# A two-layer encoder's first feed-forward matrices: one weight sum of each seven-product tile made by an adding DMA, and a fourth such tile in the second call of every group

## The chip, the core and the metric

The kernel runs on one core of a Trainium2 chip. The metric is the device time of one launch in microseconds. PE is TensorE (matmuls; PEld is its weight load), DVE is VectorE, ACT is ScalarE, POOL is GpSimd and SP is SyncE, whose queue issues the loads. A DMA issued from SP's or ACT's queue is generated in hardware, one from POOL's queue in software; the profile lists the latter as queue q0.

## The reference, cut to what matters

```python
for i in range(2):                                   # x: 256 tokens x 2048, float32
    x = x + attention_i(rms_norm(x, mixer_norm_i))   # neighbourhood, then dilated
    g, w1, w2 = ffns[i]                              # w1: 2048 x 8192, w2: 8192 x 2048
    x = x + square(relu(rms_norm(x, g) @ w1)) @ w2
return rms_norm(x, final_norm)
```

The two feed-forward layers (w1 and w2 of each) are most of the work, and the change lies in the product with w1.

## The kernel before

**Arithmetic.** Every float32 factor is split in two parts, hi and lo, both in a rounded 32-bit type: hi is ACT's cast, lo is DVE's difference of the value and hi. A product is three matmuls (`three`, L194 to L196): hi x hi, hi x lo, lo x hi, each 128x128 against 128x512.

**Calls, steps and tiles.** `gemm_pair` multiplies the 256 tokens by 1024 columns of a weight matrix in eight steps, one for each 256 rows of the weights. The step's weights lie in a tile `w` of 128 x 4 x 512: `w[:, 2:4]` are two 128-row blocks of the first 512 columns, `w[:, 0:2]` the same of the second 512. A step is of one of two kinds:
- an s step does eight block products, 24 matmuls;
- an x step treats the 2 x 2 blocks in the manner of Strassen and Winograd with seven products, 21 matmuls. It needs three sums of weight blocks more than the sum that takes a block's place, and sums of the token factor, called S1 to S4.

A feed-forward layer has four groups `g`. Each has two calls on w1 (`cp` 0 and 1, the first and the second) and two on w2. Which steps are x is written out by `ff_order`: a w1 call has x at pairs 2, 4 and 6; the first call of groups 1 to 3 (`more`) also at pair 5, in the order 0, 1, 2, 5, 3, 4, 6, 7. Calls on w2 have two to four x steps.

**Queues and their order.** The program is one long loop over the steps, in an order written out by hand; each engine runs its instructions in that order. In step i PE works through four quarters; behind quarter n the loop issues, for step i + 2, `prep(i + 2, n)`; at the end of the step SP gets the load of step i + 5, which has to wait until the tile of step i + 2, in the same buffer, has been read. There are three `w` buffers. The parts `wh` and `wl` (hi and lo) have four buffers each, two of them for a step, so that the split of step i + 2 writes where PE reads in step i.

For an s step, `prep` splits `w[:, 2:4]` at n = 1 and `w[:, 0:2]` at n = 3. For an x step `prep_x` does, in this order:
- n = 0, DVE: `sums[0:2]` from `w[1:3]` and `w[0]`, then `sums[2]`, then the sum of all four, written over `w[0]` (L166 to L168, by `add` at L137);
- n = 1: the split of `w[:, 2:4]` (ACT L189, DVE L190), whatever stands in `ahead`, and ACT's cast `hs` of all three sums (L175);
- n = 2, DVE: `ls`, the three sums less `hs` (L178, by `subtract` at L134);
- n = 3: the split of `w[:, 0:2]`.

PE's order in an x step is the list `X`: quarter 0 uses operands 2 and 3 of `s.hi` and `s.lo`, quarter 1 operands 6 and 4, quarter 2 operands 0 and 1, quarter 3 operand 5. Operands 4, 5 and 6 are `hs` and `ls`.

**What else runs beside the steps.** At the end of a call, DVE puts the seven products' sums together (`begin`, `last_sum`). After a w1 call ACT takes the squared ReLU (L790, L791), PE transposes the result in step 1 of the next call (L808), and DVE and ACT split it (`hT`) or make the sums of the token factor from it (`sums_and_parts`). After a w2 call of groups 0 to 2 a DMA from POOL's queue (`bring`, L864) adds C, 1 MB, to x in SBUF.

The adds, the split and the cast of an x step in the code before:

```python
if n == 0:
    add(nc.vector, t[:, 0:2, :], w[:, 1:3, :], w[:, 0, :] ...)
    add(nc.vector, t[:, 2, :], t[:, 1, :], w[:, 1, :])
    add(nc.vector, w[:, 0, :], t[:, 2, :], w[:, 3, :])
elif n == 1:
    split(hi, lo, w[:, 2:4, :])
    ...
    nc.scalar.copy(s.hs, s.sums)
elif n == 2:
    subtract(nc.vector, ls, s.sums, s.hs.bitcast(F32))
```

Of the kernel before, what the change touches and what calls it, by code (L numbers as in the profile page):

```python
# [8 lines left out]
F32 = mybir.dt.float32  # L9
F32R = mybir.dt.float32r  # L10
AF = mybir.ActivationFunctionType
ALU = mybir.AluOpType
AX = mybir.AxisListType

P = 128
# [13 lines left out]
class Step:  # L29
# [6 lines left out]
    def __init__(self, kind, loads, quarters):  # L36
        self.kind = kind
        self.loads = loads
        self.quarters = quarters
        self.evac = []  # L40
        self.after = [[] for _ in range(4)]
        self.tasks = [[] for _ in range(4)]
        self.post = []
        self.ahead = []
        self.hi, self.lo = [None] * 7, [None] * 7


@with_exitstack
def tile_encoder(ctx: ExitStack, tc: tile.TileContext, ins, out):
    nc = tc.nc  # L50
# [12 lines left out]
    x = const.tile([P, 2, D], F32, name="x")  # L63
# [60 lines left out]
    def load(i):  # L124
        if i >= len(steps):
            return
        s = steps[i]
        s.w = wpool.tile([P, 4, 512], F32, name="w", tag="w")
        if i:
            for src, lo, hi in s.loads:  # L130
                nc.sync.dma_start(s.w[:, lo:hi, :], src)

    def subtract(engine, out, a, b):
        engine.tensor_tensor(out=out, in0=a, in1=b, op=ALU.subtract)  # L134

    def add(engine, out, a, b):
        engine.tensor_tensor(out=out, in0=a, in1=b, op=ALU.add)  # L137

    def two_parts(s, u):
        hi = hlpool.tile([P, 2, 512], F32R, name="wh", tag="wh")  # L140
        lo = hlpool.tile([P, 2, 512], F32R, name="wl", tag="wl")
        for a in range(2):
            s.hi[2 * u + a], s.lo[2 * u + a] = hi[:, a, :], lo[:, a, :]
        return hi, lo
# [16 lines left out]
    def prep_x(s, n):  # L161

        w = s.w
        if n == 0:
            t = s.sums = part.pool.tile([P, 3, 512], F32, name="sums", tag="sums", bufs=1)
            add(nc.vector, t[:, 0:2, :], w[:, 1:3, :], w[:, 0, :].unsqueeze(1).to_broadcast([P, 2, 512]))  # L166
            add(nc.vector, t[:, 2, :], t[:, 1, :], w[:, 1, :])
            add(nc.vector, w[:, 0, :], t[:, 2, :], w[:, 3, :])  # L168
        elif n == 1:
            hi, lo = two_parts(s, 1)  # L170
            split(hi, lo, w[:, 2:4, :])
            for f in s.ahead:
                f()
            s.hs = part.pool.tile([P, 3, 512], F32R, name="hs", tag="hs", bufs=2)
            nc.scalar.copy(s.hs, s.sums)  # L175
        elif n == 2:
            ls = part.pool.tile([P, 3, 512], F32R, name="ls", tag="ls", bufs=2)
            subtract(nc.vector, ls, s.sums, s.hs.bitcast(F32))  # L178
            for a in range(3):
                s.hi[4 + a], s.lo[4 + a] = s.hs[:, a, :], ls[:, a, :]  # L180
        else:
            hi, lo = two_parts(s, 0)
            split(hi, lo, w[:, 0:2, :])
# [4 lines left out]
    def split(dst_hi, dst_lo, src):  # L188
        nc.scalar.copy(dst_hi, src)  # L189
        nc.vector.tensor_tensor(out=dst_lo, in0=src, in1=dst_hi.bitcast(F32), op=ALU.subtract)  # L190
# [88 lines left out]
    QUARTERS = (0, 0), (1, 0), (1, 1), (0, 1)  # L279
    STD = {(0, 0): "2", (0, 1): "3", (1, 0): "4", (1, 1): "S"}  # L280

    def gemm_pair(w, cols, A, sums_of, order, finish, split_end=False, soon=False, negated=False):
        made, q = [], {}
        first_x = [n for n, o in enumerate(order) if o[0] == "x"]
        touched = set()

        def left(pair, which):

            t, u = A[pair // 2], 2 * (pair % 2)
            if pair in sums_of and which in sums_of[pair]:  # L290
                return sums_of[pair][which]
            a, ts_ = {"A11": (0, 0), "A12": (1, 0), "S1": (0, 1), "A21": (0, 1), "A22": (1, 1)}[which]
            return [t[:, u + a, h, ts_ * P:(ts_ + 1) * P] for h in range(2)]

        def product(bank, a, b, last):
            if not q:
                q.update({k: banks[:, n, :] for k, n in sum_banks().items()})
            three(q[bank], a, b, bank not in touched, last)
            touched.add(bank)

        X = (("1", "A11", 2), ("2", "A12", 3), ("6", "S2", 6), ("7", "S3", 4), ("4", "A22", 0), ("3", "S4", 1),
             ("5", "S1", 5))

        for n, (kind, pair) in enumerate(order):
            k, u = pair // 2, pair % 2
            loads = [(w[k, cols[c]].rearrange("p (a n) -> p a n", n=512)[:, 2 * u:2 * u + 2, :],
                      2 - 2 * c, 4 - 2 * c) for c in (0, 1)]
            if kind == "x":
                def quarter(s, m, pair=pair, n=n):
                    for bank, a, b in X[2 * m:2 * m + 2]:  # L310
                        product(bank, left(pair, a), (s.hi[b], s.lo[b]), n == first_x[-1] and bank in "1567")
            else:
                def quarter(s, m, pair=pair, n=n):
                    tb, c = QUARTERS[m]
                    for kk in range(2):
                        b = 2 * (1 - c) + kk
                        a = (("A11", "A12"), ("A21", "A22"))[tb][kk]
                        product(STD[tb, c], left(pair, a), (s.hi[b], s.lo[b]), n == len(order) - 1 and kk == 1)
            s = Step(kind, loads, quarter)
            s.even = pair % 2 == 0  # L320
            steps.append(s)
            made.append(s)

        if split_end:
            ends = made[-2:]
            for e, s in enumerate(ends):
                def quarter(s, m, e=e):
                    tb, m = m // 2, m % 2
                    pair = order[len(order) - 2 + m][1]
                    for kk in range(2):  # L330
                        b = 2 * (1 - e) + kk
                        a = (("A11", "A12"), ("A21", "A22"))[tb][kk]
                        product(STD[tb, e], left(pair, a), (ends[m].hi[b], ends[m].lo[b]), m == 1 and kk == 1)
                s.quarters = quarter

        if made[0] is steps[0]:
            for n in range(2):
                def arriving(s, m, pair=order[n][1]):
                    if not q:
                        q.update({k: banks[:, b, :] for k, b in sum_banks().items()})  # L340
                    kk, c = m % 2, m // 2
                    u = 2 * (1 - c) + kk
                    xs = [(q[STD[tb, c]], left(pair, (("A11", "A12"), ("A21", "A22"))[tb][kk])) for tb in range(2)]
                    for o, xt in xs:
                        for h in range(2):
                            nc.tensor.matmul(o, xt[h], s.hi[u], start=steps[0] is s and kk == h == 0, stop=False)  # L346
                    for o, xt in xs:
                        nc.tensor.matmul(o, xt[0], s.lo[u], start=False, stop=False)
                    touched.update(STD[tb, c] for tb in range(2))
                made[n].quarters = arriving  # L350

        def begin(m):
            if m == 0:
                C = q["C"] = part.pool.tile([P, 4, 512], F32, name="C", tag="C")
                nc.scalar.copy(C[:, 0, :], q["1"])
                subtract(nc.vector, C[:, 1, :], q["6"], C[:, 0, :])
            elif m == 1:
                subtract(nc.vector, q["C"][:, 2, :], *(q["C"][:, 1, :], q["7"])[::-1 if negated else 1])
            elif m == 2 and negated:
                subtract(nc.vector, q["C"][:, 3, :], q["5"], q["C"][:, 2, :])  # L360
                add(nc.vector, q["C"][:, 1, :], q["C"][:, 1, :], q["5"])
            elif m == 2:
                add(nc.vector, q["C"][:, 1::2, :], q["C"][:, 1:3, :], q["5"].unsqueeze(1).to_broadcast([P, 2, 512]))

        for m in range(3 if first_x else 0):
            s = made[first_x[-1] + 1]
            s.after[0 if s is made[-1] else min(m, 1) if soon else m].append(lambda m=m: begin(m))
        finish(made, q)
        return made
# [409 lines left out]
    def ffn(norm, w1, w2, next_norm, next_done):  # L779
        for g in range(4):  # L780
# [57 lines left out]
                    at(i + 1, pe, post, quarter=r)  # L838

            for cp in range(2):  # L840
                more = g and not cp
                order = ff_order(FF_PAIRS + FF_KEPT, (0, 1, 2, 5, 3, 4, 6, 7)) if more else ff_order(FF_PAIRS)
                gemm_pair(w1, (4 * g + 2 * cp, 4 * g + 2 * cp + 1), norm.xT, norm.sums, order, lambda made, q, cp=cp: hidden(made, q, cp))

            w2g = w2[4 * g:4 * (g + 1)]

# [508 lines left out]
```

## Time and profile before

| | |
|---|---|
| time, median of 3 runs | 2239.33 us (2238.48 to 2239.36) |
| profiled execution: its time, its span | 2239.06 us, 2237.3 us |
| clock granted to TensorE | 0.999 |
| busy, share of the span: PE, PEld, DVE, ACT, POOL | 99%, 84%, 87%, 58%, 1% |
| x steps in all (casts `hs`, L175) | 113, 1482 ns each |
| software queue q0 | 12 transfers (`bring`), 12.58 MB |
| loads from HBM | 426.38 MB, 192 GB/s over the span |

How to read it: busy time is that of an engine's instructions, which can overlap a little on one engine, since the next begins while the last drains. A matmul's end is modelled, so a row of 0.39 us for a matmul says nothing of how often one starts; the starts of successive rows do. Idle time in brackets stands with the instruction that began after it, with the engine and line that released it. The windows give busy time in stretches of the span. The feed-forward layers run from about 397 to 1070 us and from about 1553 us to the end.

### The profile page before, as it was taken

Reading aid. Unit: us, or ns where it says so; the run is one execution under the profiler, and the core shown is the slowest. Engines: PE = TensorE matmul, PEld = TensorE weight load, DVE = VectorE, ACT = ScalarE, POOL = GpSimd, SP = SyncE. Lnnn points to the kernel's source line nnn. Section 1 sums busy time; section 2 is a strip of 40 time slices with the busy share of each in tenths; the row PEclk is TensorE's granted clock in tenths of the full one; section 3 lists DMA queues with packets and bytes.
Section 4 is the critical chain, followed back from the end, with each engine's and each line's share of the span. In section 5 each row is a group of like instructions: output and inputs, shape, how many; then the busy total and the mean of one; then the engine's idle time right before and its main releaser. Section 6 shows DMA issues by size and latency. Waiting matters only on the chain.

```text
span 2237.3 us, 28532 instructions
## 1 busy us (share of the span) xinstructions
PE 2225.4 (99%) x10855; PEld 1875.5 (84%) x10855; DVE 1957.0 (87%) x2324; ACT 1306.3 (58%) x1641; POOL 15.2 (1%) x18
## 2 busy tenths in 40 slices
PE   9999999999999999999999999999999999999998
PEld 7888888888888888888888888888888888888886
DVE  6978776999999999989987787767999999999988
ACT  7555555665665665565554454356665665665664
POOL 0000000000000000000000000000000000000000
PEclk9999999999999999999999999999999999999999
DMA  7566654556756756755655454444557657657663
GB/s 265 197 193 177 182 175 169 188 188 220 232 188 217 235 188 213 239 184 186 210 195 195 170 186 163 169 170 150 203 206 222 209 205 223 210 202 225 215 216 138
DMA packets 119707, 442.93 MB, mean 198 GB/s; under 512 B 24657, under 2 KB 26257, under 8 KB 105105
## 3 DMA queue, kind: packets, MB, share of 16 engines
q1 hardware_dynamic: 115776, 426.85, 55.9%
q0 software_dynamic: 3264, 12.58, 2.8%
q8 instruction: 85, 1.39, 0.3%
q10 hardware_dynamic: 528, 1.67, 0.2%
q14 instruction: 54, 0.43, 0.1%
HBM read 426.38 MB, written 2.10 MB: 192 GB/s over the span
## 4 chain that ended last, share of the span: by engine, by line
PE 99%; DVE 1%; ACT 0%; DMA 0%; issue 0%; SPq 0%; ACTq 0%; POOL 0%; POOLq 0%
PE banks L196 25%; PE banks L194 25%; PE banks L195 25%; PE banks L216 13%; PE banks L221 7%; PE banks L808 1%; PE banks L400 1%; PE banks L1030 0%; PE banks L982 0%; PE banks L669 0%; DMA x<-in_x_dram 0%; DVE wl L190 0%; PE banks L346 0%; PE banks L1009 0%; PE banks L1007 0%; PE banks L1215 0%
## 5 line engine op out<-in xcount | busy, mean ns | idle before, releaser
L190 DVE TENSOR_TENSOR wl<-w,wh 128x1024 fp32r<-128x1024 f32 (+1 forms) x803 | 961.3, 1215 | 157.6 <-ACT wh L189 106.8
L189 ACT CAST wh<-w 128x1024 fp32r<-128x1024 f32 (+1 forms) x803 | 822.4, 1047 | 374.0 <-PE banks L196 234.2
L194 PE MATMUL banks<-wh,xT 128*128 128x512 f32 x1013 | 399.1, 394 | 0.0
L196 PE MATMUL banks<-wh,xT 128*128 128x512 f32 x1013 | 394.9, 390 | 0.6 <-DVE xT L134 0.6
L195 PE MATMUL banks<-wl,xT 128*128 128x512 f32 x1013 | 394.5, 389 | 0.3 <-DVE wl L190 0.3
L216 PE MATMUL banks<-xT,wh 128*128 128x512 f32 x1280 | 310.5, 392 | 0.0
L194 PE MATMUL banks<-wh,hT 128*128 128x512 f32 x774 | 304.5, 393 | 0.0
L175 ACT CAST hs<-sums 128x1536 fp32r<-128x1536 f32 x113 | 167.5, 1482 | 232.8 <-DVE sums L137 232.8
L196 PE MATMUL banks<-wh,hT 128*128 128x512 f32 x774 | 301.6, 390 | 0.0
L195 PE MATMUL banks<-wl,hT 128*128 128x512 f32 x774 | 301.2, 389 | 0.0
L216 PEld LDWEIGHTS banks<-xT,wh 128*128 128x128 f32 x1280 | 233.9, 188 | 44.6
L196 PEld LDWEIGHTS banks<-wh,xT 128*128 128x128 f32 x1013 | 190.1, 188 | 40.8 <-DVE xT L134 1.0
L195 PEld LDWEIGHTS banks<-wl,xT 128*128 128x128 f32 x1013 | 190.4, 188 | 38.9 <-DVE wl L190 1.2
L194 PEld LDWEIGHTS banks<-wh,xT 128*128 128x128 f32 x1013 | 190.3, 188 | 37.7
L134 DVE TENSOR_TENSOR ls<-sums,hs 128x1536 fp32r<-128x1536 f32 x113 | 197.9, 1752 | 12.4 <-ACT hs L175 12.4
L196 PEld LDWEIGHTS banks<-wh,hT 128*128 128x128 f32 x774 | 145.3, 188 | 30.6
L221 PE MATMUL banks<-xT,wl 128*128 128x256 f32 x1280 | 170.7, 284 | 0.0
L195 PEld LDWEIGHTS banks<-wl,hT 128*128 128x128 f32 x774 | 145.4, 188 | 29.1
L194 PEld LDWEIGHTS banks<-wh,hT 128*128 128x128 f32 x774 | 145.4, 188 | 28.7
L221 PEld LDWEIGHTS banks<-xT,wl 128*128 128x128 f32 x1280 | 164.3, 191 | 5.0
L137 DVE TENSOR_TENSOR sums<-w 128x1024 f32<-128x1024 f32 x113 | 137.6, 1217 | 0.0
L137 DVE TENSOR_TENSOR sums<-sums,w 128x512 f32<-128x512 f32 x113 | 78.2, 692 | 3.9
(225 smaller groups left out, 2535.3 us busy)
## 6 DMA issues: line engine op xcount, KB each, us to landing
w<-in_ffn_w_dram SPq DMA_DIRECT2D x512, 512.0 KB, 4.4
w<-in_dil_wqkv_dram SPq DMA_DIRECT2D x56, 1024.0 KB, 4.8
w<-in_na_wqkv_dram SPq DMA_DIRECT2D x32, 1024.0 KB, 5.0
w<-in_na_wo_dram SPq DMA_DIRECT2D x16, 1024.0 KB, 4.8
w<-in_dil_wqkv_dram SPq DMA_DIRECT2D x32, 512.0 KB, 4.4
w<-in_na_wqkv_dram SPq DMA_DIRECT2D x29, 512.0 KB, 5.2
x<-C POOLq DMA_DIRECT2D x12, 1024.0 KB, 11.8
w<-in_dil_wo_dram SPq DMA_DIRECT2D x8, 1024.0 KB, 4.7
```

What stands on the lines that cost most here:

```text
L134: engine.tensor_tensor(out=out, in0=a, in1=b, op=ALU.subtract)
L137: engine.tensor_tensor(out=out, in0=a, in1=b, op=ALU.add)
L175: nc.scalar.copy(s.hs, s.sums)
L189: nc.scalar.copy(dst_hi, src)
L190: nc.vector.tensor_tensor(out=dst_lo, in0=src, in1=dst_hi.bitcast(F32), op=ALU.subtract)
L194: nc.tensor.matmul(o, left[0], right[0], start=start, stop=False)
L195: nc.tensor.matmul(o, left[0], right[1], start=False, stop=False)
L196: nc.tensor.matmul(o, left[1], right[0], start=False, stop=stop)
L216: nc.tensor.matmul(acc[j // 2][:, j % 2, :], s.hi[a][:, j * P:(j + 1) * P], xT[k][:, a].rearrange("p h t -> p (h t)"), start=k == 0 and a ...
L221: nc.tensor.matmul(acc[j // 2][:, j % 2, :T], s.lo[a][:, j * P:(j + 1) * P], xT[k][:, a, 0, :], start=False, stop=k == nk - 1 and a == 3)
L400: nc.tensor.transpose(self.tp[:, a, tb * P:(tb + 1) * P], x[:, tb, kt * P:(kt + 1) * P], ident)
L808: nc.tensor.transpose(t[:, a, tb * P:(tb + 1) * P], q["C"][:, 2 * tb + f // 4, f % 4 * P:(f % 4 + 1) * P], ident)
```

## The change

In the two calls on w1 of each group, the x steps are `added` steps:
- SP loads `w[:, 0:2]` ahead of `w[:, 2:4]` (before, the other way round), and a DMA from POOL's queue adds `w[1]` to `w[0]` in SBUF, 128 x 512 float32 or 256 KB, once the first load is there;
- DVE makes three sums of 128x512 from it: `sums[2]` = `w[0]` + `w[2]`, `sums[1]` = `sums[2]` - `w[1]`, `sums[0]` = `sums[2]` + `w[3]`. They stand at n = 1 behind the split of `w[:, 2:4]` and ahead of `hs`; at n = 0 nothing is left;
- the sum of all four is now `sums[0]` (operand 4), and the sum of two is the new `w[0]` (operand 0), so PE takes operands 0 and 4 in exchanged places;
- the second w1 call of every group has four x steps in place of three, in the order that the first call of groups 1 to 3 has. That makes four more x steps in each layer: 31 of 64 w1 steps in place of 27.

The steps on w2, on the attention matrices and the first call of group 0 keep their kinds and order.

```diff
@@ load
-            for src, lo, hi in s.loads:
+            for src, lo, hi in s.loads[::-1 if s.added else 1]:
                 nc.sync.dma_start(s.w[:, lo:hi, :], src)
+            if s.added:
+                nc.gpsimd.dma_start(s.w[:, 0, :], s.w[:, 1, :], accum_op=ALU.add)
@@ prep_x
-        if n == 0:
+        if s.added and n < 2:
+            if n == 0:
+                return
+            hi, lo = two_parts(s, 1)
+            split(hi, lo, w[:, 2:4, :])
+            t = s.sums = part.pool.tile([P, 3, 512], F32, name="sums", tag="sums", bufs=1)
+            add(nc.vector, t[:, 2, :], w[:, 0, :], w[:, 2, :])
+            subtract(nc.vector, t[:, 1, :], t[:, 2, :], w[:, 1, :])
+            add(nc.vector, t[:, 0, :], t[:, 2, :], w[:, 3, :])
+            for f in s.ahead:
+                f()
+            s.hs = part.pool.tile([P, 3, 512], F32R, name="hs", tag="hs", bufs=2)
+            nc.scalar.copy(s.hs, s.sums)
+        elif n == 0:
@@ gemm_pair
                     for bank, a, b in X[2 * m:2 * m + 2]:
+                        b = {0: 4, 4: 0}.get(b, b) if s.added else b
...
+            s.added = added and kind == "x"
@@ ffn
-                more = g and not cp
+                more = g or cp
                 order = ff_order(FF_PAIRS + FF_KEPT, (0, 1, 2, 5, 3, 4, 6, 7)) if more else ff_order(FF_PAIRS)
-                gemm_pair(w1, ..., lambda made, q, cp=cp: hidden(made, q, cp))
+                gemm_pair(w1, ..., lambda made, q, cp=cp: hidden(made, q, cp), added=True)
```

More of the change, by code (lines that the diff above doesn't have):

```diff
@@ L45, in __init__ @@
         self.hi, self.lo = [None] * 7, [None] * 7
+        self.added = False
 @with_exitstack
@@ L280, in tile_encoder, with gemm_pair @@
     STD = {(0, 0): "2", (0, 1): "3", (1, 0): "4", (1, 1): "S"}
-    def gemm_pair(w, cols, A, sums_of, order, finish, split_end=False, soon=False, negated=False):
+    def gemm_pair(w, cols, A, sums_of, order, finish, split_end=False, soon=False, negated=False, added=False):
         made, q = [], {}
@@ L840, in ffn @@
             for cp in range(2):
-                more = g and not cp
+                more = g or cp
                 order = ff_order(FF_PAIRS + FF_KEPT, (0, 1, 2, 5, 3, 4, 6, 7)) if more else ff_order(FF_PAIRS)
-                gemm_pair(w1, (4 * g + 2 * cp, 4 * g + 2 * cp + 1), norm.xT, norm.sums, order, lambda made, q, cp=cp: hidden(made, q, cp))
+                gemm_pair(w1, (4 * g + 2 * cp, 4 * g + 2 * cp + 1), norm.xT, norm.sums, order, lambda made, q, cp=cp: hidden(made, q, cp),
+                          added=True)
             w2g = w2[4 * g:4 * (g + 1)]
```

## The prediction

> **What bounds the kernel now.** I read the page first: engines, slices, chain.
>
> ```profile
> span 2237.3 us, 28532 instructions
> PE 2225.4 (99%) x10855; PEld 1875.5 (84%) x10855; DVE 1957.0 (87%) x2324; ACT 1306.3 (58%) x1641; POOL 15.2 (1%) x18
> DVE  6978776999999999989987787767999999999988
> ...
> PE 99%; DVE 1%; ACT 0%; DMA 0%; issue 0%; SPq 0%; ACTq 0%; POOL 0%; POOLq 0%
> ```
>
> TensorE sets the end, and VectorE is at nine tenths or more through both feed-forward layers, which the change touches. The windows cut at the calls (first w1 call of group 0; then a second w1 call, two w2 calls and the next group's first w1 call), and last the stretch from the second w1 call of group 0 to that of group 3 in each layer, say which has room. Columns: length, then busy time of PE, PEld, DVE, ACT, POOL.
>
> ```profile
> 397.30:437.35 40.05, 40.05 (x182) 33.25 (x181) 36.66 (x47) 24.46 (x28) 0.00 (x0) 1.00 0.60 207
> ...
> 605.70:649.10 43.40, 43.40 (x201) 35.86 (x200) 40.33 (x46) 29.51 (x37) 0.00 (x0) 1.00 0.54 193
> 649.10:692.35 43.25, 43.25 (x201) 35.82 (x200) 42.12 (x51) 29.78 (x38) 0.00 (x0) 1.00 0.59 204
> 692.35:733.20 40.85, 40.85 (x182) 33.84 (x181) 40.14 (x42) 22.45 (x22) 1.20 (x1) 1.00 0.71 221
> 733.20:774.05 40.85, 40.85 (x182) 33.84 (x181) 40.03 (x40) 22.43 (x22) 1.20 (x1) 1.00 0.73 228
> ...
> 437.35:985.80 548.45, 548.45 (x2475) 453.95 (x2474) 527.76 (x569) 341.40 (x380) 7.33 (x6) 1.00 0.64 211
> ...
> 1593.10:2141.60 548.50, 548.50 (x2475) 454.04 (x2474) 527.67 (x569) 341.39 (x380) 7.20 (x6) 1.00 0.63 210
> ```
>
> PE never stops and its clock is granted in full (1.00). DVE idles 3.07, 1.13, 0.71 and 0.82 us in the last four of these calls: 5.7 us of a group's 168.35, 20.7 us of a layer's 548.45. So PE bounds, and DVE is 3.4% behind it. The call from 733.20 holds four x tiles and four s tiles: 4 x 21 + 4 x 24 = 180 matmuls in 40.85 us, 0.227 us each. An x tile is 4.76 us of PE, an s tile 5.44.
>
> What a tile costs DVE is read from the timeline, start to start, since independent instructions overlap.
>
> ```profile
> 619.82 1.23 DVE L190 TENSOR_TENSOR wl<-w,wh 128x1024 fp32r<-128x1024 f32 x1 [0.53 <-ACT wh L189]
> 620.97 1.22 DVE L137 TENSOR_TENSOR sums<-w 128x1024 f32<-128x1024 f32 x1
> 622.22 0.69 DVE L137 TENSOR_TENSOR sums<-sums,w 128x512 f32<-128x512 f32 x1
> 622.94 0.69 DVE L137 TENSOR_TENSOR w<-sums,w 128x512 f32<-128x512 f32 x1
> 623.55 1.22 DVE L190 TENSOR_TENSOR wl<-w,wh 128x1024 fp32r<-128x1024 f32 x1
> 624.69 1.75 DVE L134 TENSOR_TENSOR ls<-sums,hs 128x1536 fp32r<-128x1536 f32 x1
> 626.36 1.22 DVE L190 TENSOR_TENSOR wl<-w,wh 128x1024 fp32r<-128x1024 f32 x1
> 627.49 1.07 DVE L134 TENSOR_TENSOR h<-h 128x256 f32<-128x256 f32 x3
> ...
> 630.10 2.36 DVE L190 TENSOR_TENSOR wl<-w,wh 128x1024 fp32r<-128x1024 f32 x2 [0.28 <-ACT wh L189]
> ...
> 641.50 4.63 DVE L190 TENSOR_TENSOR wl<-w,wh 128x1024 fp32r<-128x1024 f32 x4 [0.34 <-ACT wh L189]
> 646.05 0.68 DVE L134 TENSOR_TENSOR C<-banks,C 128x512 f32<-128x512 f32 x1
> ```
>
> An x tile takes 620.97 to 627.49 = 6.52 us of DVE, an s tile half of 641.50 to 646.05 = 2.28. DVE loses 1.76 us on PE with each x tile and wins 3.16 with each s tile.
>
> **The change part by part.**
> - Four more x tiles a layer (second w1 call of each group): 8 x 3 = 24 matmuls go, 24 x 0.227 = 5.4 us of PE, 2.7 a layer, all on the path as long as PE stays the bound.
> - The DMA's sum. One DVE add goes, a 128x1024 (1.25 us) becomes a 128x512, in 31 w1 x tiles a layer (3 + 7 x 4).
> - The order. The adds move from n = 0 to n = 1, behind the split of the tile's second half, because they now wait for the DMA. This is the costly part. hs (ACT) reads all three sums and ls (DVE) reads hs; on DVE nothing stands between the last add and ls. Before, that split stood between.
>
> ```profile
> 622.94 1.49 ACT L175 CAST hs<-sums 128x1536 fp32r<-128x1536 f32 x1 [2.20 <-DVE sums L137]
> ...
> DVE ls L134 <- ACT hs L175: 12.4, 16, 1.3
> ```
>
> The wait list's last row: over all 113 x tiles DVE waited 12.4 us for hs, in 16 of them. Now each of the 62 waits in full. New x tile on DVE: split 1.13, adds 0.72 + 0.61 + 0.69, 0.03 to ACT, hs 1.49, 0.03 back, ls 1.67, split 1.13: 7.50 us. DVE is busy 0.5 us less and tied up 0.98 us more. Each new x tile costs 7.50 - 2.28 = 5.22 us.
>
> How far DVE is ahead shows where ls ends against the first matmul that reads hs:
>
> ```profile
> 571.94 1.75 DVE L134 TENSOR_TENSOR ls<-sums,hs 128x1536 fp32r<-128x1536 f32 x1
> ...
> 576.77 0.39 PE L194 MATMUL banks<-hs,xs 128*128 128x512 f32 x1
> ...
> 593.79 1.75 DVE L134 TENSOR_TENSOR ls<-sums,hs 128x1536 fp32r<-128x1536 f32 x1
> ...
> 596.49 0.39 PE L194 MATMUL banks<-hs,xs 128*128 128x512 f32 x1
> ...
> 614.07 1.76 DVE L134 TENSOR_TENSOR ls<-sums,hs 128x1536 fp32r<-128x1536 f32 x1 [1.31 <-ACT hs L175]
> ...
> 616.88 0.68 DVE L190 TENSOR_TENSOR hT<-banks,hT 128x512 fp32r<-128x512 f32 x1
> 617.48 1.21 DVE L190 TENSOR_TENSOR wl<-w,wh 128x1024 fp32r<-128x1024 f32 x1
> ...
> 619.45 0.40 PE L194 MATMUL banks<-hs,xs 128*128 128x512 f32 x1
> ...
> 658.26 0.58 ACT L189 CAST hT<-banks 128x512 fp32r<-128x512 f32 x1
> ```
>
> In the first w1 call the lead is 576.77 - 573.69 = 3.1 us at step 2 and 596.49 - 595.54 = 0.95 at step 6. The sums give that fall: DVE does three x and one s (3 x 6.52 + 2.28 = 21.84) while PE does steps 2 to 5 (3 x 4.76 + 5.44 = 19.72): 2.1. The second w1 call starts with 3.6. The lead cannot grow: a tile's split waits for PE to leave the buffers of the tile two steps before.
>
> After, with the same count:
> - First call: 3 x 7.50 + 2.28 = 24.8 against 19.7, short by 5.1, of which a lead of 3.0 covers part. The swap of operands 0 and 4 asks for the last split one product (0.68 us) after ls, and that split ends 1.2 after it: 0.5 more. Stall 2.6 us.
> - Second call, x now at steps 2, 3, 5, 6: the same, plus two hT pieces (616.88 to 617.48, 0.6 each) and one set of sums of the other factor (627.49 to the next split, 630.10 less its wait of 0.28: 2.3), plus 0.5, as the hT piece between the adds and ls waits for an ACT copy (0.58) queued behind hs: 28.8 against 19.7, short by 9.1; minus 3.6, plus 0.5: stall 6.0 us.
>
> The w2 calls keep their order and costs; their 1.8 us of idle refill the lead. A layer loses 4 x 6.0 + 3 x 2.6 = 31.8 us (the first call of group 0 keeps three x tiles and has 40.05 - 36.66 = 3.4 of idle), wins 2.7: +29.1, for two layers +58.2. The profiled execution took 2239.06 us (span 2237.3), 0.3 below the median of 2239.33: 2239.1 + 58.2 = 2297.3.
>
> Bounds: if every idle microsecond of DVE can be used, a layer has 24 x 0.98 + 4 x 5.22 = 44.4 us more work, less 20.7 idle, less a lead of 3.6: about 20, or 2279. With no lead at all, 4 x 9.1 + 3 x 5.1 - 2.7 = 49 a layer, or 2337.
>
> **The DMA itself.** No row shows a 256 KB adding DMA; the nearest are these (median us from issue to landing; POOL's own row last):
>
> ```profile
> w<-in_ffn_w_dram SPq DMA_DIRECT2D x512, 512.0 KB, 4.4
> ...
> x<-C POOLq DMA_DIRECT2D x12, 1024.0 KB, 11.8
> ...
> out_dram<-x SPq DMA_DIRECT2D x8, 256.0 KB, 2.5
> ...
> L864 POOL DMA_DIRECT2D x<-C x2 | 2.4, 1200 | 165.9 <-DVE x L137 165.9
> ...
> 621.08 0.33 SPq L131 DMA_DIRECT2D w<-in_ffn_w_dram  x1
> ...
> 632.38 1.22 DVE L137 TENSOR_TENSOR sums<-w 128x1024 f32<-128x1024 f32 x1
> ```
>
> A load is issued when the tile three before it is split, and the adds came 632.38 - 621.08 = 11.3 us later; now they come behind a split, 12.4. Shortest is the room at steps 5 and 6 of a first call, one x tile, one s tile and a split, 7.50 + 2.28 + 1.13 = 10.9; step 2, behind two s tiles and the closing sums of a call, has much the same. The sum is ready 4.4 + 2.5 to 4.4 + 11.8 us after the load: 6.9 to 16.2. I take the middle of the landings, 7: ready at 11.4, late by half a microsecond at worst, and charge nothing; the upper end is a rival. A gain is excluded: nothing else starts sooner for it.
>
> The Trainium skill (DMA: Bandwidth & Descriptors, Anatomy of one DMA — SWDGE (gpsimd) path) fits such a DMA as 2.0 us plus its bytes at 436 GB/s. By that, an estimate, 256 KB would land in 2.6 us, the sum be ready at 7.0, and rival 2 below fall away, with the sum at 2297 as before. The same fit makes 4.4 us of the 1 MB transfer that took 11.8 here, so the measurement decides and that rival keeps its chance.
>
> At nothing: POOL gains 62 issues of 1.2 us beside 15.2 busy. A bring (x<-C) may queue there behind a sum waiting for its load, some 5 us; C is next written 35 us later. The reversed loads bring the second half one issue (0.4 us) later, with some 10 us of room. SP's and ACT's queues wait for the same DVE work as before. If DVE's tie-up were gone, these would still be covered.
>
> **The rivals.**
> 1. DVE keeps up and PE's saving is all there is: 2239.1 - 5.4 = 2233.6. For it: DVE's busy time falls by 31 x 0.5 a layer, about what four more x tiles add. It decides if the wait for hs is filled; then a tile costs 5.95 and the second call is short by 28.8 - 4.65 - 0.5 - 19.7 = 3.9, about the lead. Against: nothing stands in DVE's queue there. 12 in 100; a partial cover that ends within 0.2% (4.5 us, about what a measurement of this kernel can tell from no change), 5.
> 2. The sum comes late, and DVE waits twice, for the DMA and for hs. At a landing near 8.5 to 9.5 us it is 2 to 3 late in about half of the 62 tiles: +62, 2359; at the full 11.8, 31 x 4.2 = +130, 2427. For it: the 11.8, taken under a DVE as busy as here. Against: a quarter of the bytes. 18 in 100.
>
> **How the numbers follow.** Forecast 2297, 65 in 100. Slower by over 0.2% are forecast and rival 2: 83; same 5; faster 12. The range 2265 to 2365 reaches from below the full-use bound, with part of the wait covered, over the no-lead bound to the milder case of rival 2; left out are rival 1, no change, and the far end of rival 2 (3): 20.
>
> **What would show it.** ls idle before it for ACT hs: about 1.5 us x 62, some 95 us against 12.4, while DVE's busy time hardly moves. Gaps between matmuls at L194 and L195 on ls and wl in the w1 calls, none in w2 calls. Windows: second w1 call about 43.4 - 0.7 + 6.0, first about +2.6, w2 unchanged. No or little DVE wait for a DMA on w. It is wrong if ls doesn't wait, or if DVE's adds wait for POOL's DMA.

## The result, and the profile after

The changed kernel took 2349.16 us (median of 5 runs, 2348.32 to 2351.78), the kernel before 2239.14 beside it: a ratio of 1.0495 [1.0483, 1.0507], 110.0 us slower.

The page of the changed kernel (lines are shifted: `hs` is L179, or L191 in steps that are not added; `ls` L137, `add` L140, a split ACT L205 and DVE L206, the three matmuls L210 to L212):

```profile
span 2346.5 us, 28896 instructions
PE 2265.7 (97%) x10831; PEld 1881.0 (80%) x10831; DVE 1957.2 (83%) x2356; ACT 1315.5 (56%) x1649; POOL 69.2 (3%) x80
DVE  6877767899899789879987786758899799799788
...
PE 4%; DVE 1%; ACT 0%; issue 0%; ACTq 0%
...
w<-in_ffn_w_dram SPq DMA_DIRECT2D x512, 512.0 KB, 4.7
...
w<-w POOLq DMA_DIRECT2D x62, 256.0 KB, 4.3
...
x<-C POOLq DMA_DIRECT2D x12, 1024.0 KB, 12.5
```

24 matmuls are gone and DVE is as busy as before (1957.2 against 1957.0), yet the span is 109.2 us longer. Of that, 68.9 us is PE standing idle (2346.5 - 2265.7 = 80.8 against 2237.3 - 2225.4 = 11.9); 40.3 us is PE "busier" with less work, which is a row's length after a stop and a slower clock, shown below. The chain of waits breaks off early this time (its shares add up to 5%), so it can't be used; the windows and the wait list carry the reading.

Windows of the kernel after: the first w1 call of group 0, a second w1 call, a w2 call, the next group's first w1 call; then a second w1 call of the next group, the second of its w2 calls and the first w1 call after them. Columns: length, busy PE, PEld, DVE, ACT, POOL, granted clock, DMA share, GB/s.

```profile
397.30:439.20 41.90, 40.78 (x181) 32.65 (x180) 33.57 (x45) 23.55 (x27) 1.72 (x2) 1.00 0.59 188
439.20:491.80 52.60, 45.99 (x198) 36.22 (x196) 42.68 (x51) 31.07 (x37) 3.43 (x4) 0.97 0.60 181
491.80:535.05 43.25, 43.25 (x200) 35.86 (x199) 42.40 (x51) 30.05 (x37) 0.00 (x0) 1.00 0.58 209
...
575.90:620.70 44.80, 42.35 (x182) 33.55 (x182) 38.02 (x40) 22.00 (x21) 4.03 (x5) 1.00 0.81 233
620.70:673.20 52.50, 45.94 (x198) 36.17 (x197) 41.84 (x50) 31.07 (x37) 3.43 (x4) 0.97 0.59 176
...
716.45:757.30 40.85, 40.85 (x181) 33.81 (x181) 40.33 (x42) 22.35 (x21) 1.61 (x2) 1.00 0.74 232
757.30:805.10 47.80, 44.36 (x181) 34.46 (x180) 37.91 (x40) 22.09 (x21) 4.34 (x5) 0.96 0.77 221
```

All the loss is in the w1 calls: a second call is 52.5 long where it was 43.4 (+9.1, although it has three matmuls less), a first one 44.8 to 47.8 where it was 40.85, the first of group 0 41.9 where it was 40.05. The w2 calls have not moved by a hundredth. In the second calls DVE has some 10 us free (52.5 - 42): it is not short of time, it waits.

What the waits are for (wait list: engine and line, what it waited for, us in total, times, longest):

```profile
DVE ls L137 <- ACT hs L179: 80.4, 52, 1.6
PE banks L210 <- DVE hT L206: 35.5, 18, 4.1
PE banks L211 <- DVE ls L137: 20.7, 21, 1.3
DVE hT L206 <- ACT hT L205: 16.2, 8, 2.0
PE banks L211 <- DVE wl L206: 10.2, 32, 1.0
DVE sums L140 <- issue: 3.2, 1, 3.2
```

DVE's wait for `hs` was forecast, and so were PE's waits for `ls` and `wl`. The largest of PE's waits, 35.5 us for `hT`, was not. The last row is all that DVE waited at the adds that read the DMA's sum. The timeline of DVE and ACT in step 1 of a second w1 call, with the added tile of step 3:

```profile
448.66 1.76 DVE L137 TENSOR_TENSOR ls<-sums,hs 128x1536 fp32r<-128x1536 f32 x1 [1.55 <-ACT hs L179]
...
453.21 0.68 DVE L140 TENSOR_TENSOR sums<-w 128x512 f32<-128x512 f32 x1
453.93 0.69 DVE L137 TENSOR_TENSOR sums<-sums,w 128x512 f32<-128x512 f32 x1
454.54 0.68 DVE L140 TENSOR_TENSOR sums<-sums,w 128x512 f32<-128x512 f32 x1
455.25 1.47 ACT L179 CAST hs<-sums 128x1536 fp32r<-128x1536 f32 x1 [4.25 <-DVE sums L140]
456.63 0.58 ACT L205 CAST hT<-banks 128x512 fp32r<-128x512 f32 x1
457.24 0.69 DVE L206 TENSOR_TENSOR hT<-banks,hT 128x512 fp32r<-128x512 f32 x1 [2.02 <-ACT hT L205]
457.85 1.75 DVE L137 TENSOR_TENSOR ls<-sums,hs 128x1536 fp32r<-128x1536 f32 x1
```

and PE across it:

```profile
453.48 0.40 PE L212 MATMUL banks<-wh,xT 128*128 128x512 f32 x1
457.99 0.51 PE L210 MATMUL banks<-hs,xs 128*128 128x512 f32 x1 [4.12 <-DVE hT L206]
458.33 0.60 PE L211 MATMUL banks<-ls,xs 128*128 128x512 f32 x1
458.72 0.63 PE L212 MATMUL banks<-hs,xs 128*128 128x512 f32 x1
459.15 0.63 PE L210 MATMUL banks<-wh,xs 128*128 128x512 f32 x1
```

PE's third product of step 2, the first that reads `hs` (`hs` by `xs`), waits for `hT`, which it does not read: it needs the PSUM bank. Step 1 transposes the hidden activations in four pieces r = 0 to 3 into the spare banks; step 2's products take those banks as they come free. The bank of r = 0 or 1 is free when ACT has cast the piece and DVE has taken the difference. In the changed kernel that DVE instruction (here of r = 1) stands behind the split and the three adds of step 3's tile, and its ACT cast behind `hs`: 453.2 to 457.9 on DVE, while PE needed the bank at 453.7. In the kernel before, the same DVE instruction and the one behind it read:

```profile
618.61 0.68 DVE L190 TENSOR_TENSOR hT<-banks,hT 128x512 fp32r<-128x512 f32 x1
619.82 1.23 DVE L190 TENSOR_TENSOR wl<-w,wh 128x1024 fp32r<-128x1024 f32 x1 [0.53 <-ACT wh L189]
```

The bank came free at 619.29, and PE's product began at 619.45: 0.16 us of room, at the row from which I read a lead of 3.6.

After the stop PE's rows are 0.43 apart (458.72, 459.15) in place of 0.23. Windows of the kernel after, before, in and behind the stop, and further on; the third column from the end is the granted clock:

```profile
450.00:453.70 3.70, 3.54 (x19) 2.55 (x16) 3.70 (x5) 1.01 (x2) 0.00 (x0) 1.00 0.28 72
453.70:458.00 4.30, 0.18 (x2) 0.01 (x1) 2.24 (x5) 2.75 (x4) 0.86 (x1) 1.00 0.70 212
458.00:461.70 3.70, 3.70 (x9) 2.92 (x10) 3.70 (x3) 2.08 (x3) 0.00 (x0) 0.55 0.23 40
461.70:465.00 3.30, 3.30 (x16) 2.72 (x15) 1.40 (x3) 1.05 (x1) 0.00 (x0) 0.99 0.96 271
```

Nine matmuls in 3.7 us, then sixteen in 3.3: a stop of 4.3 us costs nearly 2 more. Counted over the starts of the 128x512 matmuls of the feed-forward layers, stops take 95 us and 89 matmuls at half rate 18; less the 5.4 saved, that is 108 of the 109 of the span. By calls, from the start of one to the start of the next: a second call loses about 10 before its saving (4.3 in the bank's stop, 1.2 to 2 at the half rate, some 3.4 in later stops for `ls` and `wl`), eight of them 81; a first call of groups 1 to 3 3.7 to 7.0, six of them 27; the first calls of group 0 2.2 and 3.9.

### The profile page after: what moved, and what is told of

It is laid out like the page before. It is cut to its first block, busy times and chain, and to the rows that moved or that the text cites. A ratio compares the mean times of both kernels' runs of the same rounds, so it can differ in the third digit from the quotient of the medians.

```text
span 2346.5 us, 28896 instructions
## 1 busy us (share of the span) xinstructions
PE 2265.7 (97%) x10831; PEld 1881.0 (80%) x10831; DVE 1957.2 (83%) x2356; ACT 1315.5 (56%) x1649; POOL 69.2 (3%) x80
## 5 line engine op out<-in xcount | busy, mean ns | idle before, releaser
L206 DVE TENSOR_TENSOR wl<-w,wh 128x1024 fp32r<-128x1024 f32 (+1 forms) x803 | 958.1, 1216 | 176.1 <-ACT wh L205 124.6
L205 ACT CAST wh<-w 128x1024 fp32r<-128x1024 f32 (+1 forms) x803 | 819.2, 1046 | 369.7 <-PE banks L212 211.9
L210 PE MATMUL banks<-wh,xT 128*128 128x512 f32 x911 | 359.7, 395 | 1.3 <-DVE hT L206 1.3
L211 PE MATMUL banks<-wl,xT 128*128 128x512 f32 x911 | 355.7, 390 | 4.6 <-DVE wl L206 4.4
L212 PE MATMUL banks<-wh,xT 128*128 128x512 f32 x911 | 355.2, 390 | 0.6 <-DVE xT L137 0.6
L210 PE MATMUL banks<-wh,hT 128*128 128x512 f32 x774 | 304.5, 393 | 0.0
L212 PE MATMUL banks<-wh,hT 128*128 128x512 f32 x774 | 301.6, 390 | 0.0
L137 DVE TENSOR_TENSOR ls<-sums,hs 128x1536 fp32r<-128x1536 f32 x121 | 212.3, 1755 | 81.3 <-ACT hs L179 80.4
L179 ACT CAST hs<-sums 128x1536 fp32r<-128x1536 f32 x62 | 91.7, 1479 | 218.7 <-DVE sums L140 218.7
L211 PEld LDWEIGHTS banks<-wl,xT 128*128 128x128 f32 x911 | 171.2, 188 | 41.2 <-DVE wl L206 7.6
L210 PEld LDWEIGHTS banks<-wh,xT 128*128 128x128 f32 x911 | 171.1, 188 | 37.5 <-DVE hT L206 3.2
L212 PEld LDWEIGHTS banks<-wh,xT 128*128 128x128 f32 x911 | 171.0, 188 | 36.8 <-DVE xT L137 1.0
L212 PEld LDWEIGHTS banks<-wh,hT 128*128 128x128 f32 x774 | 145.3, 188 | 30.4
L210 PEld LDWEIGHTS banks<-wh,hT 128*128 128x128 f32 x774 | 145.3, 188 | 28.9
L191 ACT CAST hs<-sums 128x1536 fp32r<-128x1536 f32 x59 | 87.5, 1483 | 131.3 <-DVE sums L140 131.3
L140 DVE TENSOR_TENSOR sums<-w 128x512 f32<-128x512 f32 (+1 forms) x121 | 114.3, 945 | 3.6 <-issue 3.2
## 6 DMA issues: line engine op xcount, KB each, us to landing
x<-C POOLq DMA_DIRECT2D x12, 1024.0 KB, 12.5
```

What stands on the lines that cost most here:

```text
L210: nc.tensor.matmul(o, left[0], right[0], start=start, stop=False)
L211: nc.tensor.matmul(o, left[0], right[1], start=False, stop=False)
L212: nc.tensor.matmul(o, left[1], right[0], start=False, stop=stop)
```

## The experiments

My theory after this (A in the expectations): the place of the adds costs twice, once by DVE's wait for `hs` and once by the banks of step 1. The rivals: the fourth x tile is too much for DVE wherever the adds stand (B); and the DMA (late, or its traffic, or the queue of POOL) costs by itself (C; D where it is the late sum alone). All times are in us; the kernel before had 2238.9 to 2239.3 beside each set.

| run | what it is | median | ratio to before [95%] |
|---|---|---|---|
| e3_tile_only | before, with the fourth tile | 2274.8 | 1.0158 [1.0144, 1.0171] |
| e4_three_tiles | after, without the fourth tile | 2289.4 | 1.0222 [1.0208, 1.0237] |
| e14_order_no_dma | before, adds of w1 tiles behind the split | 2279.6 | 1.0178 [1.0165, 1.0192] |
| e15_no_sums | after, without the three adds | 2237.4 | 0.9993 [0.9984, 1.0002] |
| e1_adds_first | after, adds at n = 0 | 2301.5 | 1.0276 [1.0262, 1.0291] |
| e2_hT_first | after, `hT` ahead of the tile | 2338.0 | 1.0439 [1.0424, 1.0453] |
| e5_both | e1 and e2 | 2294.1 | 1.0243 [1.0229, 1.0257] |
| e10_plain_order | after, x at 2, 4, 5, 6 in second calls | 2325.7 | 1.0387 [1.0373, 1.0401] |
| e11_plain_no_dma | e3 in that order | 2264.8 | 1.0114 [1.0097, 1.0131] |
| e12_plain_room | e11 with the DMA's sum at two steps | 2262.8 | 1.0106 [1.0091, 1.0121] |
| e9_first_calls | the DMA's sum in first calls alone | 2274.6 | 1.0161 [1.0147, 1.0175] |
| e8_where_room | the DMA's sum at three steps of second calls | 2260.7 | 1.0099 [1.0085, 1.0112] |

### One part alone: the tile, the order, the DMA

**e3_tile_only**, the kernel before with

```diff
-                more = g and not cp
+                more = g or cp
```

> The kernel before with the fourth x tile in every second w1 call, and nothing else of the change (no adding DMA, loads and operands as before, adds at n = 0 on DVE). Theory A: by DVE's sums an x tile is 6.52 us; from step 2 to step 6 DVE needs 3 x 6.52 + 2.28 + 3.5 = 25.3 against PE's 19.7, with 3.6 of lead, so some 2 us short, and hT comes some 2.8 us late: 3 to 5 us in each of eight calls, less 5.4: 2258 to 2274. Theory B (the tile is the cost): near the changed kernel, 2330 or more. Theory C (the DMA is the cost): 2234 to 2240, since without the DMA the fourth tile pays.

It cost 35.5 us, just above the range. Its wait list:

```profile
PE banks L194 <- DVE hT L190: 16.5, 9, 2.0
DVE ls L134 <- ACT hs L175: 11.6, 16, 1.3
PE banks L195 <- DVE wl L190: 4.8, 8, 0.8
```

The wait for `hs` is as small as before (12.4), and yet PE stops for the bank of `hT`, some 2 us in each second call: an x tile at step 3 (an s tile before) already delays `hT` in step 1, without any other change. In the prediction these 24 matmuls stood as a gain.

**e4_three_tiles**, the changed kernel with

```diff
-                more = g or cp
+                more = g and not cp
```

> The changed kernel without its fourth x tile in the second calls (three x tiles in the old order, steps 2, 4, 6); the adding DMA and the adds behind the split stay in all 54 w1 x tiles. Theory A (the place of the adds ties DVE up, and in step 1 of a second call holds the PSUM banks of the transposes): step 1 prepares an s tile again, so no stop of 4.3 us; DVE waits some 1.5 us for hs in each of 54 tiles; the first calls of groups 1 to 3 lose the 3.7 us that they lose in the changed kernel, six times: 2239 + 22 = about 2261, between 2252 and 2268. Theory B (the fourth tile alone is the cost): 2239 or less.

It cost 50.5, far more than expected. By calls, 33 us of that are lost in the first calls of groups 1 to 3, which have four x tiles in every version; the calls with three x tiles lose 1.4 each (second calls) and 2.2 and 3.8 (first calls of group 0). The full wait for `hs` is there (80.5 us in 52), and PE hardly waits for `hT` (1.3 us): without an x tile at step 3 the bank's stop is gone. The tile on top of the order therefore costs 110.0 - 50.5 = 59.5, against 35.5 alone: the two parts make each other worse, all of it in the second calls, which are 76 us longer in the changed kernel, 35 in e3 and 11 in e4.

**e14_order_no_dma**, the kernel before with the adds of the w1 x tiles behind the split; four sums on DVE, no DMA, no fourth tile:

```diff
+        if s.added and n == 0:
+            return
+        if s.added and n == 1:
+            hi, lo = two_parts(s, 1)
+            split(hi, lo, w[:, 2:4, :])
-        if n == 0:
+        if n == int(s.added):
...
```

> The kernel before with one edit: in the w1 calls the x tiles' adds (all of them on DVE, as before) stand at n = 1 behind the split of the tile's second half. No adding DMA, no reversed loads, no exchanged operands, no fourth tile. Theory A (the place of the adds is the cost, as DVE then stands for hs): an x tile ties DVE up 8.15 us in place of 6.52, 0.6 more than in the changed kernel; so at least what the changed kernel without its fourth tile lost (50 us), and some 4 us more in each of eight groups: 2289 + 35 = 2324, between 2300 and 2345. Theory C (the DMA, its traffic or the reversed loads make the 50 us of that run): 2239 to 2260.

It cost 40.5, less than expected, since I had miscounted one thing: here `hs` does not read the last add (that goes to `w[0]`), so the wait for it is half as long:

```profile
DVE ls L135 <- ACT hs L184: 42.9, 53, 0.8
```

The wait is shorter and the adds longer by the fourth; the tile comes to 7.43 us on DVE (443.21 to 450.64), much the 7.50 of the prediction. So 40 of e4's 50 are the place of the adds, with no DMA in the kernel. The time falls between the two ranges that were expected. The other 10 lie in three calls of e4: DVE waits 7.8 us at its first add in three tiles, one in each of three first calls of groups 1 to 3, and these lose 8.5, 6.9 and 6.2 where the other three lose 3.7 each, 10.4 more in sum. They are late sums of the DMA. An effect of operands 0 and 4 in exchanged places can't be told from nothing here.

**e15_no_sums**, the changed kernel with the three adds left out; the sums are missing from its result, and `hs` casts three weight blocks instead. The DMA, POOL's queue, the reversed loads and the fourth tile are all there:

```diff
-            t = s.sums = part.pool.tile([P, 3, 512], F32, name="sums", tag="sums", bufs=1)
-            add(nc.vector, t[:, 2, :], w[:, 0, :], w[:, 2, :])
-            subtract(nc.vector, t[:, 1, :], t[:, 2, :], w[:, 1, :])
-            add(nc.vector, t[:, 0, :], t[:, 2, :], w[:, 3, :])
+            s.sums = w[:, 1:4, :]
```

> The changed kernel with the three DVE adds of its x tiles left out: hs and ls are made of three quarters of the weight tile itself, so the three sums of the seven products are missing from the result. All else stays: the adding DMA, the reversed loads, the fourth tile, the exchanged operands. hs no longer waits for DVE; an x tile costs DVE 1.13 + 1.67 + 1.13 = 3.9 us. Theory A: PE is the bound again and shows what the change has to win: 2239 - 5.4 = 2234, between 2232 and 2237. Theory C (the DMA's traffic, POOL's queue or the loads cost something themselves): above 2242.

It ended at 2237.4, 0.4 above what was expected and not to be told from the kernel before:

```profile
span 2235.9 us, 28711 instructions
PE 2221.2 (99%) x10831; PEld 1870.4 (84%) x10831; DVE 1844.5 (82%) x2170; ACT 1318.9 (59%) x1649; POOL 69.1 (3%) x80
```

With DVE 113 us less busy and nothing between it and `hs`, PE is back at 99%, and the traffic of 62 adding DMAs and POOL's queue cost a microsecond or two at most. PE's saving is real (2221.2 against 2225.4 busy), and it is small: of the 5.4, 1.7 reach the time, and 2.6 go in two waits for the bank of `hT` in the second calls of the last groups. What costs is DVE's work and its order, not the DMA's traffic or POOL's queue. Whether a sum comes late is not tested here: nothing reads `w[0]` before the last split.

### Taking the waits away

**e1_adds_first**, the changed kernel with the three adds back at n = 0, ahead of the split:

```diff
         if s.added and n < 2:
             if n == 0:
+                t = s.sums = ...          # and the three adds, moved up from below
                 return
```

> The changed kernel with its three adds back at n = 0, ahead of the split, as the kernel before has them; the adding DMA, the exchanged operands and the fourth x tile stay. Theory A (the place of the adds costs the time: DVE stands for hs in each x tile, and the first-matrix result hT, queued behind that wait in step 1 of a second call, keeps a PSUM bank that PE needs): DVE's wait for hs falls from 80 us to under 15, an x tile takes DVE 5.9 us, and what is left is hT coming some 1.5 us late in the eight second calls, so 2239 - 5 + 12 = about 2246, between 2234 and 2255. Theory B (the fourth tile is too much for DVE, wherever the adds stand): some 2300 or more. Theory C (the adding DMA is the cost: late sums, or slower loads): the adds now ask for the sum 1.1 us sooner, so DVE waits for POOL's DMA and the time is above 2349.

It won 47.7 of the 110, not all of them, and came to where theory B had put it; but the wait list shows late sums, the mechanism of C. The wait for `hs` fell from 80.4 to 24.0, and another took its place:

```profile
DVE sums L140 <- DMA w<-w: 28.3, 15, 7.2
DVE sums L140 <- issue: 26.6, 4, 6.9
DVE ls L137 <- ACT hs L179: 24.0, 50, 2.0
PE banks L211 <- DVE wl L206: 26.1, 20, 4.0
```

At n = 0 DVE comes for the sum before the DMA has made it ("issue" is a wait for which the trace shows no releaser; it stands at the same instruction, L140). For step 5 of a first call the load and the sum have only a tile of 6.4 and one of 2.28 us to land in, and in the median the load takes 4.6 and the sum 5.1 more (more still in this place, see e9). The wait passes on to the last split, `wl`, and to PE.

**e2_hT_first**, the changed kernel; in quarter 1, if the tile of step i + 2 is an added one, step 1's `hT` is issued ahead of `prep`:

```diff
+            ahead = n == 1 and i + 2 < len(steps) and steps[i + 2].added
+            if ahead:
+                for pe, post in s.tasks[n]:
+                    post()
             if i > 2 and n < 3:
                 prep(i + 2, n)
-            for pe, post in s.tasks[n]:
+            for pe, post in () if ahead else s.tasks[n]:
                 post()
```

> The changed kernel, with one difference: where a step has PE transposes behind its quarter 1 and prepares an added tile (step 1 of each second w1 call), the split of the transposed block (hT, ACT cast and DVE difference) is issued ahead of that tile's preparation in place of behind it. Theory A: PE's stop of 4.3 us ahead of the first product of step 2, eight times, goes, and with it the matmuls at half rate (427 ns) that follow it there; DVE is still tied up 7.5 us by an x tile, so part of it returns later in the call: 2300 to 2320. Theory B or C: the stop moves to the next product that waits for a split or a sum, and the time stays at 2340 to 2355.

It won 11 us where at least 29 were expected. The stop went on to the next bank:

```profile
458.14 0.80 PE L210 MATMUL banks<-wh,xs 128*128 128x512 f32 x1 [3.31 <-ACT h L835]
```

Piece r = 2 is copied out of its bank by ACT (`h`, L835), and that copy still stands behind `hs`. So a bank's release can be held by DVE's adds or by ACT's cast behind them; freeing one moves the stop to the other.

**e5_both**, e1 and e2 together:

> The changed kernel with both edits: adds at n = 0 and hT ahead of the preparation in step 1 of a second call. Theory A: no PE stop is left but small ones, PE's 24 matmuls less are the whole difference: 2234 to 2237, the first version below the kernel before. Theory B: above 2260. Theory C: above 2300, with DVE waiting for the DMA.

It missed theory A's range by 57. It is 7.4 better than e1; what is left is the DMA's lateness (DVE waits 34.0 us for it in 17 tiles and 20.0 more at "issue"), above all in the first calls, and the piece r = 0, now behind the adds at n = 0.

**e10_plain_order**, the changed kernel with the second calls' steps in order, x at 2, 4, 5, 6, so that an s tile is prepared in step 1:

```diff
-                order = ff_order(FF_PAIRS + FF_KEPT, (0, 1, 2, 5, 3, 4, 6, 7)) if more else ff_order(FF_PAIRS)
+                order = ff_order(FF_PAIRS + FF_KEPT, range(8) if cp else (0, 1, 2, 5, 3, 4, 6, 7)) if more else ff_order(FF_PAIRS)
```

> The changed kernel with the second calls' steps in plain order, so that the four x tiles lie in steps 2, 4, 5 and 6 and step 1 prepares an s tile. Theory A: hT no longer stands behind a wait for hs; the stop of 4.3 us and the half-rate matmuls behind it (1.2 us) go in eight calls, of which some comes back in steps 5 and 6, where three x tiles follow one another: 2300 to 2325, and under 20 us of PE waiting for hT against 77 in the changed kernel's two rows. If the stop is only DVE's lack of time (theory B), it moves to a later step of the same call: 2340 to 2352.

It won 23.4 of the 110 (0.7 above the range of theory A). PE's wait for `hT` fell from 35.5 to 1.3 us, which is the share of step 1's banks; with three x tiles in a row PE now stops at steps 5 and 6, and its wait for `ls` rose from 20.7 to 29.2. So the bank's stop goes when step 1 prepares an s tile, with as many x tiles as before; the 23.4 are what that brings less what the three x tiles in a row cost.

**e11_plain_no_dma**, e3 with the same edit of the order; no DMA, the adds at n = 0 as in the kernel before:

> The kernel before with a fourth x tile in the second calls, in plain order (x in steps 2, 4, 5 and 6), no adding DMA. It differs from the run of the tile alone (2274.8 us) only in step 1, which prepares an s tile. Theory A (the PSUM banks of the transposes, held while step 1 prepares an x tile, make most of that run's 35 us): the stop ahead of step 2 goes; DVE is short by 25.3 - 19.7 - 3.6 = 2 us in each second call: 2239 + 16 - 5 = 2250, between 2243 and 2260. Theory B (the tile is too much for DVE wherever it lies): 2268 to 2280.

It is 10 better than e3 and still 25.7 slower than before, between the ranges of A and B. No bank is late; DVE is:

```profile
472.72 0.49 PE L195 MATMUL banks<-wl,xT 128*128 128x512 f32 x1 [1.15 <-DVE wl L190]
```

Before the saving, six of the eight second calls lose 4.6 us in such stops, the two of group 3 1.7. A fourth x tile does not fit the lead that DVE has, in either order.

### Where there is room for the sum

**e12_plain_room**, e11 with the DMA's sum at steps 4 and 6 of second calls (the adds at n = 0):

```diff
-            s.added = added and kind == "x"
+            s.added = n in added and kind == "x"
...
+                          added=(4, 6) if cp else ())
```

> As the run without a DMA in plain order, and in addition the adding DMA for the tiles of steps 4 and 6 of the second calls, with the adds at n = 0; there the sum has some 10 us from the load on. Theory A: DVE's short is 24.0 - 19.7 - 3.6 = 0.7 us in a call, so 2239 + 6 - 5 = 2240, between 2234 and 2247, and some 10 us below the run without a DMA. If sums are late there too (theory D): at or above that run.

DVE never waits for the DMA, and only 2 us are won: two adds of 0.6 less a call against stops of over 4. Neither theory has this: the sums are in time, and it is no 10 us better.

**e9_first_calls**, e1 with the DMA's sum in first calls alone, and three tiles in second calls:

```diff
-                more = g or cp
+                more = g and not cp
-                          added=True)
+                          added=not cp)
```

> The kernel before with the adding DMA in the first w1 calls only, adds at n = 0 (three sums of 512 elements, loads turned round); second calls as before, with three x tiles and no DMA sum. DVE does less work than before and hT is not touched. Theory D (with the adds at n = 0 the sum comes late where x tiles lie close, in steps 5 and 6 of the first calls of groups 1 to 3): DVE waits 6 to 8 us for POOL's DMA once or twice in each of six calls and PE stops some 5 us in each: 2262 to 2275. If the DMA sum only takes work off DVE: 2237 to 2240.

As expected. DVE is 15.5 us less busy than in the kernel before (1941.5), and the kernel is 35.7 slower: in ten of its 30 added tiles DVE stands 44 us waiting for the sum. One of them on the timeline:

```profile
567.62 1.35 POOL L883 DMA_DIRECT2D x<-C  x1
...
581.53 0.91 POOL L134 DMA_DIRECT2D w<-w  x1 [12.56 <-DVE wl L206]
...
589.90 0.69 DVE L140 TENSOR_TENSOR sums<-w 128x512 f32<-128x512 f32 x1 [6.15 <-issue]
...
593.11 0.79 PE L211 MATMUL banks<-wl,xT 128*128 128x512 f32 x1 [2.46 <-DVE wl L206]
```

The sum is issued at 581.5, and DVE can begin at 589.9, 8 us later. The 1 MB `bring` ahead of it in POOL's queue is not what holds it: by the trace it had landed at 580.0. The loads are beside it: two of 512 KB, issued by SP at 581.5 and 581.9, landed at 586.4 and 588.0. So it is in each of the six first calls of groups 1 to 3: the sum of step 5 took 8.3 to 9.9 us to land, with no `bring` under way and 1.7 to 2.1 MB of loads moved meanwhile; the three quickest of this run, with less than 0.1 MB of loads, took 3.3.

**e8_where_room**, four tiles with the order of the changed kernel, the DMA's sum only at steps 3, 5 and 6 of second calls, the adds at n = 0, and `hT` ahead of `prep` in quarters 0 and 1:

```diff
+            s.added = n in added and kind == "x"
+            s.first = bool(added) and n == 3
...
-                          added=True)
+                          added=(3, 5, 6) if cp else ())
```

> The fourth x tile in all second calls; adds at n = 0; the adding DMA only for the tiles of steps 3, 5 and 6 of a second call, where by the trace of the version with both edits the sum lands before DVE asks for it; all other x tiles as in the kernel before; in step 1 of a second call hT is split ahead of the preparation, in quarters 0 and 1. Theory A, with late sums as a second cause: no PE stop of more than a microsecond, 2234 to 2240. If the fourth tile is too much for DVE in itself (theory B): 2255 or more.

The fastest but e15, which leaves the sums out, and still 21.8 slower than before, in theory B's range. DVE does not wait for the DMA, and for the added tiles' `hs` only 5.1 us; PE still stops for the banks (9.1 us for `hT`, 2.6 for ACT's copy) and for `wl` (4.6). So no kernel with the whole product came below the kernel before.

## Why the prediction held, and where its sum was short

The forecast was 2297, the range 2265 to 2365, slower in 83 of 100; it came to 2349. It is slower by the mechanism that was forecast; that 2349 lies within the range is partly luck. The range went beyond 2337, the bound of this mechanism without any lead, only for the sake of rival 2, late sums, and the one late sum of the changed kernel cost 3.2 us. By its steps:

- **The tile on DVE, 7.50 us**: right. In the timeline of the kernel after, from one split of an x tile at 443.96 to the next instruction at 451.48 it is 7.52. e14, without a DMA, has 7.43.
- **`ls` waits for `hs`, some 95 us, DVE as busy as before**: right. 80.4, and 16.2 in the eight tiles in which `hT` stands between and waits in its place; e2, which moves `hT` away, has 95.9 in all 62.
- **The DMA charged with nothing**: right at n = 1, for a reason half seen. The landing was 4.3, not the 7 I took, and DVE waited 3.2 us in one tile; in e4, with the adds in the same place, three sums were late and cost 10. e1, e5 and e9 show the rival in full: with the adds one split and more earlier the sum is late by up to 7.8 us. The adds had a choice of two waits, for ACT behind the split or for the DMA ahead of it.
- **PE's 5.4 saved**: there (e15: 4.2 less busy), and lost many times over. The tile's own cost on DVE stood in the sum, but the prediction never priced the tile alone; e3 has it at 35.5.
- **w2 unchanged, stops on `ls` and `wl` in w1 calls**: right, to a hundredth of a microsecond.
- **The step that was mis-sized is the lead.** I put the stall of a second call at 6.0, with a lead of 3.6 taken off, and the runs have 10.1. The first calls of groups 1 to 3 stood at 2.6, measured 4.6 on average; the first of group 0 at nothing, measured 2.2 and 3.9. In sum 8 x 4.1 + 6 x 2.0 + 6.1 = 51, against the 52 by which the forecast was short. A lead was read from one producer, `ls`, to one reader. PE's product needs its operands and also a bank, and the bank's lead was 0.16 us. I had priced `hT` as 0.6 us of DVE's time and a wait of 0.5, and not as something that PE waits for. Once PE has stopped for it, DVE's lead on the operands has bought nothing; e2 (the stop moves to the next bank) and e10 (it goes when step 1 prepares an s tile, and 23 us with it, 2.9 of the 4.1 a call) show that part. In the first calls, which have no `hT`, the runs don't separate what of the 2.0 is lead and what each stop adds by itself: the call from 575.90 has five stops of 2.45 us together in the brackets of PE's rows, and is 3.95 longer.
- **The clock was left out.** My bound with no lead at all was 2337; the kernel went 12 beyond. The 18 us at the half rate, which a sum of waits doesn't hold, are more than that.

Between the parts: the place of the adds 40 (e14), with three late sums of the DMA 50 (e4), the fourth tile 35 alone (e3) and 60 on top of the others, of which 23 go when the tile stands elsewhere (e10). A version with more weight buffers, which would give the sum longer to land, was not tried.

## What to carry to other kernels

A lead is the smallest over everything that an instruction waits for, buffers and PSUM banks too: before an order is changed, list who frees each bank that PE opens next, and what will now stand ahead of it on ACT and DVE. An operation that is handed from a busy engine to a DMA saves its time only if the rest can start as late as the DMA ends; in e4 DVE was 29 us less busy than before (1927.6 against 1957.0) and the kernel lost 50. And where an engine is 3% behind the bound, a trade of 0.68 us on PE for 4.24 on that engine (an x tile for an s tile in the kernel before), as the fourth tile makes, has to be tried alone first: e3, one line, held a third of the loss.

## What the runs showed of the hardware that I had not expected

**A stop of TensorE can be paid twice.** The granted clock was 0.55 in the 3.7 us behind a stop of 4.3, and matmuls began every 0.43 us in place of 0.227. The Trainium skill (TensorE: Matmul & The Clock Gate, What's actually happening) has the clock at half after an idle window of about 3.4 us, and the window running freely. For the second half of this the trace's record of the clock agrees: from the first half-rate stretch, at 458.36, to the last in the feed-forward layers, all are 3.41 or 6.83 us long, and their starts lie whole multiples of 3.413 us apart, to within 3 ns, whatever the stops between. The window need not be idle throughout, though: the half rate follows where no stop was that long. Rows of PE in the kernel after:

```profile
786.62 0.51 PE L210 MATMUL banks<-hs,xs 128*128 128x512 f32 x1 [0.55 <-ACT hs L179]
788.41 0.51 PE L211 MATMUL banks<-ls,xs 128*128 128x512 f32 x1 [1.29 <-DVE ls L137]
...
790.56 0.63 PE L210 MATMUL banks<-hs,xT 128*128 128x512 f32 x1
790.99 0.63 PE L211 MATMUL banks<-ls,xT 128*128 128x512 f32 x1
```

Two stops of 0.55 and 1.29 us, close together, were followed by a stretch at 0.43 a matmul. A similar pair in an earlier call (0.16 and 1.30 at 609 to 611) was not. Cut into the windows of 3.413 us, the first pair falls in a window (786.04 to 789.45) with 2.5 us beyond the 0.227 that each matmul takes, the other in one (608.55 to 611.96) with 2.0. Counted so in the feed-forward layers of the changed kernel and of the twelve experiments, the 58 full-rate windows that a half-rate one followed had 2.05 us or more, and of the others none had over 2.15. So in these runs about 2.1 us of waiting in one window, in one stop or in several, halve the clock of the next.

**An adding DMA inside SBUF is slow for its size.** 256 KB landed in 4.3 us (median of 62), 1 MB in 12.5, and in other orders the median of the 256 KB was 4.2 to 5.7. The quickest of the changed kernel took 3.2, and beside loads from HBM it was 8 and more (e9). The estimate of 2.6 us that the prediction worked out from the Trainium skill (DMA: Bandwidth & Descriptors, Anatomy of one DMA — SWDGE (gpsimd) path) does not hold here, nor does the 7 that I took.
